# A decoder kernel on one core: the compressed turns placed behind a projection, and part of the first layer's output projection placed ahead of the memory's output

## The chip, the cores and the metric

The kernel runs on one core of one Trainium2 chip. The metric is the time of one execution on the device, in microseconds (us). The kernel before took 633.94 us in the median of three runs (633.56 to 634.37).

The core's engines work through instruction queues of their own, each in order, and wait for each other by semaphores. The profile calls them PE (matrix products; PEld is its loading of weights), DVE (vector), ACT (scalar functions and copies), POOL and SP (which here issues the DMAs).

## The reference: what is computed

Two decoder layers over 256 tokens of width 1024. Each layer has a token mixer, a cross-attention with 4 heads into 256 memory tokens, one output projection of both, and a SwiGLU feed-forward part. The first layer's mixer is a gated MLP; the second's is an attention with three branches.

```python
for i in range(2):
    h, mem_n = rmsnorm(x, norm_mix[i]), rmsnorm(mem, norm_mem[i])
    mix, mem_q = gmlp_mixer(h, ...) if i % 2 == 0 else nsa_mixer(h, ...)
    mem_o = mem_cross_attention(mem_q, mem_n, w_mem_kv[i])      # 4 heads of 64: 256 columns
    x = x + jnp.concatenate([mix, mem_o], axis=-1) @ w_out      # (768 + 256) x 1024
    x = x + swiglu(rmsnorm(x, norm_ffn[i]), wg, wu, wd)
return rmsnorm(x, norm_final)

# nsa_mixer, a head (12 heads of 64, 4 key heads), with softmax p and gate g of each branch:
o = g0 * (p_c @ v_compressed) + g1 * (p_s @ v_selected) + g2 * (p_w @ v_window)
```

With 256 tokens the selected and the window branch both see every earlier position, and the compressed branch sees 15 blocks of keys.

## The kernel before, in words

All matrix products of weights are made three times: a value is held as a rounded high part H and a rest L, and `mm3` (lines 226 to 232) issues H times H (L229), L times H (L230) and H times L (L231). One such triple of 128 rows by 512 columns is called a k-product below. H is made by ACT and L by DVE from the same source (`split`, lines 122 to 124): the L of an activation cannot be made before its H, and the k-product's second matmul needs it. Row tile `tb` is tokens 0 to 127 or 128 to 255.

Weights come through three raw buffers (`Raw`, one DMA from SP each) and seven pairs wH, wL of one piece each; a new piece is cast when the k-product that frees an older one has been recorded (`Stream.pump`). PE's order is the order of the code. Side work is a generator in a heap of due times (`Flow`): `flow.spawn` and each `yield` name a delay, a k-product moves the clock by its estimated length (line 232), and what is due is recorded next. `MEMLAT` is the delay between the scores of the memory attention and the turning of its probabilities. The order on DVE, ACT, POOL and SP is set by a scheduler from the order of the code and from priorities (`tc.high_priority`).

First layer, lines 681 to 707. `v_chain` (lines 650 to 679) makes the mixer's output and turns it for PE (`gm`, L673, transposed by L245). The memory attention (`mem_attention`, lines 382 to 426) runs once per row tile: scores on PE (L389), maxima on DVE (L393), exponentials on ACT (L401), a scaling on POOL (L406), eight transposes on PE (L245), copies on ACT (L414), the products with the values on PE (L422), and the split into the projection's k = 6, 7 (L123 on ACT, L124 on DVE). The output projection `down` (lines 309 to 320) takes k = 0 to 3 for both row tiles and both halves of the columns, waits in the recording until both memory attentions are recorded (line 705), then takes k = 4 to 7. A finished half of a row tile starts `f0.chain` (lines 299 to 303: residual L307, transposes, gain L280, split, squares L250), which the feed-forward part needs.

Second layer, lines 918 to 1074. The 12 heads are taken in six steps m = 0 to 5 of two heads. `scores(m)` needs four of the four PSUM buffers called `tr`; it is followed by masks and maxima on DVE (L945, L947), exponentials on ACT (L951, L963) and the scaling on POOL (L956). `turn(m)` transposes the probabilities of both heads (12 transposes, L245, three `tr` buffers, copied out by ACT at L976 and L982) and then the compressed branch's (`pcx`, one transpose, a fourth `tr` buffer, copied by ACT at L985). `attend(m)` multiplies with the values (L1003), the compressed ones last in each row tile, into a `tr` buffer `o`, which is split for the projection. Between them `mixed` takes pieces (m, tb) of the output projection: two k-products each, k = m, one row tile, both halves. After (5, tb) the chain `f1.chain` is started, and the feed-forward part follows.

Of the kernel before, what the change touches and what calls it, by code (L numbers as in the profile page):

```python
# [58 lines left out]

HI = 150  # L60
UP = 500
MEMLAT = 9.0
MEMCH = 0.0
VCH = 2.0
WARM, WARM2 = 6, 2
# [3 lines left out]
def body(tc, t, out):  # L69
    nc = tc.nc  # L70
    PE, ACT, DVE, POOL, SP = nc.tensor, nc.scalar, nc.vector, nc.gpsimd, nc.sync
    with ExitStack() as ctx:
# [236 lines left out]
        def down(accs, act, ks, ws, first, last, after=None, tbs=(0, 1)):  # L309

            for tb in tbs:
                for half in range(2):
                    acc = accs[tb][half]
                    for i, k in enumerate(ks):
                        mm3(acc, st(act, k, tb), ws[i](slice(half * 512, (half + 1) * 512)),
                            first and i == 0, last and i == len(ks) - 1)
                        if tb == 1 and half == 1:
                            ws[i].done()
                    if after:
                        after(acc, tb, half)  # L320
# [329 lines left out]
        def v_chain():  # L650
            POOL.affine_select(wsr, wsr, pattern=[[0, 12], [-1, 128]], compare_op=ALU.is_ge, fill=0.0, base=0, channel_multiplier=1)
            for tb in range(2):
                ss = tiny([128, 2], "ss")
                sumsq(Vv[:, tb, 0:512], ss[:, 0:1], GW)
                sumsq(Vv[:, tb, 512:768], ss[:, 1:2], GW)
                r = rstd_of(ss)
                yield 1.5
                DVE.scalar_tensor_tensor(Vv[:, tb, :], Vv[:, tb, :], r, vg, op0=ALU.mult, op1=ALU.mult)
            yield 2.0
            for q in range(3):  # L660
                ps = tr()
                transposes(ps, wsr[:, q * 4 : q * 4 + 4, :].rearrange("p g s -> p (g s)"), 4)
                ACT.copy(wsT[:, q * 4 : q * 4 + 4, :], kview(ps, 4))
                yield 0.8 if q < 2 else 2.4
            for q in range(3):
                spatial(q)
                yield 1.0
            for c, n in ((0, 512), (512, 256)):
                for tb in range(2):
                    while tb not in u_done:  # L670
                        yield 0.3
                    gm = small([128, n])
                    DVE.tensor_tensor(gm, U[:, tb, c : c + n], Vv[:, tb, c : c + n], op=ALU.mult)  # L673
                    yield 1.0
                    ps = tr()
                    transposes(ps, gm, n // 128)
                    k = c // 128
                    split(mix[0][:, k : k + n // 128, blk(tb)], mix[1][:, k : k + n // 128, blk(tb)], kview(ps, n // 128))
            v_done.append(1)
# [16 lines left out]
        kv0 = mem_kv(WK0)  # L696
        flow.until(lambda: None not in qT0)
        for tb in range(2):
            flow.spawn(mem_attention(qT0, tb, kv0, mix, mo_done), 1.0 + 5.5 * tb)
        flow.until(lambda: v_done)  # L700
        early.close()
        f0 = Norm(gT[:, FFN : FFN + 8])
        accs = [[mm(), mm()], [mm(), mm()]]
        down(accs, mix, [0, 1, 2, 3], WO0[0] + WO0[1], True, False)
        flow.until(lambda: len(mo_done) == 2)
        down(accs, mix, [4, 5, 6, 7], WO0[2] + WO0[3], False, True,
             lambda *a: flow.spawn(f0.chain(*a)))
        flow.until(lambda: f0.rstd[0] is not None)
        n1 = Norm(gT[:, MIX + 8 : MIX + 16])
        ffn(WF0, f0, n1.chain)  # L710
# [259 lines left out]
        def turn(m):  # L970
            ps = soft[m]
            t0 = tr()
            for hh in range(2):
                transposes(t0, ps[hh], 2, hh * 2)
            pT0 = mid([128, 4, 128])
            ACT.copy(pT0, kview(t0, 4))  # L976
            pT1 = []
            for hh in range(2):
                t1 = tr()
                transposes(t1, ps[hh][:, 256:768], 4)  # L980
                pT1.append(mid([128, 4, 128]))
                ACT.copy(pT1[hh], kview(t1, 4))  # L982
            tc_ = tr()
            transposes(tc_, pcs[:, m % 2], 1)
            ACT.copy(pcT[:, m % 2], tc_[:, 0:128])  # L985
            turned[m] = pT0, pT1

        def attend(m):
            pT0, pT1 = turned[m]
# [26 lines left out]


        def step(f, *a):
            with tc.high_priority(offset=UP if f is turn else HI):
                f(*a)  # L1020

        ps = mm()
# [26 lines left out]
        step(scores, 1)  # L1049
        mixed((6, 1), (7, 1))  # L1050
        step(turn, 0)
        step(scores, 2)
        step(attend, 0)
        step(turn, 1)
        mixed((0, 0))
        step(scores, 3)
        step(attend, 1)
        step(turn, 2)
        mixed((1, 0))
        step(scores, 4)  # L1060
        step(attend, 2)
        step(turn, 3)
        mixed((0, 1))
        step(scores, 5)
        mixed((2, 0))
        step(attend, 3)
        step(turn, 4)
        mixed((1, 1), (3, 0))
        step(attend, 4)
        step(turn, 5)  # L1070
        mixed((2, 1), (4, 0))
        step(attend, 5)
        mixed((3, 1), (5, 0), (4, 1), (5, 1))
        flow.until(lambda: f1.rstd[0] is not None)

        nf = mid2([128, D])
# [63 lines left out]
```

## Time and profile before

| what | value |
|---|---|
| time, median of 3 runs | 633.94 us (633.56 to 634.37) |
| the profiled execution, its own time | 634.55 us |
| its span, first to last instruction | 632.8 us |
| PE busy | 618.1 us, 98% of the span |
| DVE, ACT, POOL busy | 377.1, 327.3, 58.2 us |
| granted TensorE clock, mean | 0.998 of full speed |

The span and the rows are of the one profiled execution; 1.75 us of its time lie outside its span. A timeline row has the start, the length, the engine, the line and operation, what is written from what is read, the shape, the number of merged instructions, and in brackets the engine's idle time just before and what ended it. The length of a matmul overlaps with the next one's; how long PE takes per instruction is read from one start to the next.

### The profile page before, as it was taken

The numbers are of one execution on the slowest core, as the hardware profiler recorded it, in microseconds if no ns is written. First come the engines' busy times: TensorE is split into PE (matmuls) and PEld (weight loads), VectorE is DVE, ScalarE is ACT, GpSimd is POOL, SyncE is SP. The second block draws the span as 40 slices with busy tenths as digits, with TensorE's granted clock in tenths as the row PEclk, the third lists the DMA queues.
The fourth block names the chain that finished last, engine by engine and source line by source line (L and its number), as shares of the span: only waits on it lengthen the run. The fifth ranks groups of instructions, "written<-read, shape, count | busy, mean of one in ns | idle before, by whom it ended". The sixth has DMA issues, their size and how long they took to land.

```text
span 632.8 us, 8848 instructions
## 1 busy us (share of the span) xinstructions
PE 618.1 (98%) x3382; PEld 513.9 (81%) x3382; DVE 377.1 (60%) x616; ACT 327.3 (52%) x553; POOL 58.2 (9%) x90
## 2 busy tenths in 40 slices
PE   8999999999999999999999999899999999999995
PEld 7889879888888888889886787678988888888884
DVE  3998457464554544566688479766544645446344
ACT  4885557452534434456543559766533535344423
POOL 0330121000000000002001204431000000000001
PEclk9999999999999999999999999999999999999999
DMA  7966254555546464643967742133554655647401
GB/s 244 369 217 247 75 165 169 200 172 186 177 171 225 138 261 134 241 159 87 330 201 206 193 103 65 35 121 115 198 199 134 226 173 179 220 138 235 159 1 67
DMA packets 57331, 109.69 MB, mean 173 GB/s; under 512 B 3429, under 2 KB 19401, under 8 KB 57289
## 3 DMA queue, kind: packets, MB, share of 16 engines
q1 hardware_dynamic: 57272, 109.12, 51.9%
q8 instruction: 26, 0.43, 0.3%
q14 instruction: 17, 0.13, 0.1%
q10 hardware_dynamic: 16, 0.00, 0.0%
HBM read 108.07 MB, written 1.05 MB: 172 GB/s over the span
## 4 chain that ended last, share of the span: by engine, by line
PE 90%; ACT 5%; DVE 2%; DMA 1%; issue 1%; POOL 0%; SPq 0%; POOLq 0%; ACTq 0%; DVEq 0%
PE mm L229 14%; PE mm L230 14%; PE mm L231 14%; PE tr L230 13%; PE tr L231 13%; PE tr L229 13%; PE tr L245 5%; ACT mid L951 3%; PE tr L800 1%; DMA x<-in_x_dram 1%; PE tr L389 1%; PE tr L422 1%; PE tr L1003 1%; ACT wH L123 1%; DVE wL L124 0%
## 5 line engine op out<-in xcount | busy, mean ns | idle before, releaser
L124 DVE TENSOR_TENSOR wL<-raw,wH 128x1024 fp32r<-128x1024 f32 (+1 forms) x170 | 205.5, 1228 | 149.5 <-ACT wH L123 143.8
L123 ACT CAST wH<-raw 128x1024 fp32r<-128x1024 f32 (+1 forms) x170 | 173.8, 1043 | 152.3 <-PE tr L230 75.5
L229 PE MATMUL tr<-wH,aH 128*128 128x512 f32 (+1 forms) x384 | 143.8, 375 | 0.0
L230 PE MATMUL tr<-wH,aL 128*128 128x512 f32 (+1 forms) x384 | 142.8, 372 | 0.6 <-DVE aL L124 0.6
L231 PE MATMUL tr<-wL,aH 128*128 128x512 f32 (+1 forms) x384 | 142.7, 372 | 0.0
L229 PE MATMUL mm<-wH,aH 128*128 128x512 f32 (+2 forms) x224 | 87.7, 391 | 0.0
L230 PE MATMUL mm<-wH,aL 128*128 128x512 f32 (+2 forms) x224 | 83.2, 371 | 0.0
L231 PE MATMUL mm<-wL,aH 128*128 128x512 f32 (+2 forms) x224 | 83.2, 371 | 0.0
L230 PEld LDWEIGHTS tr<-wH,aL 128*128 128x128 f32 x384 | 72.4, 188 | 13.0 <-DVE aL L124 0.9
L231 PEld LDWEIGHTS tr<-wL,aH 128*128 128x128 f32 x384 | 72.3, 188 | 12.5
L229 PEld LDWEIGHTS tr<-wH,aH 128*128 128x128 f32 x384 | 72.3, 188 | 12.3
L229 PE MATMUL mm<-wH,mid 128*128 128x512 f32 (+1 forms) x208 | 79.2, 381 | 0.0
L230 PE MATMUL mm<-wH,mid 128*128 128x512 f32 (+1 forms) x208 | 77.9, 374 | 0.0
L231 PE MATMUL mm<-wL,mid 128*128 128x512 f32 (+1 forms) x208 | 77.8, 374 | 0.0
L229 PEld LDWEIGHTS mm<-wH,aH 128*128 128x128 f32 x224 | 42.9, 191 | 9.6 <-issue 4.0
L231 PEld LDWEIGHTS mm<-wL,aH 128*128 128x128 f32 x224 | 42.6, 190 | 7.4
L258 POOL TENSOR_SCALAR rstd<-ss 128x1 f32<-128x1 f32 x14 | 8.0, 575 | 434.6 <-ACT junk L250 430.5
L230 PEld LDWEIGHTS mm<-wH,aL 128*128 128x128 f32 x224 | 42.7, 191 | 5.6
L231 PEld LDWEIGHTS mm<-wL,mid 128*128 128x128 f32 x208 | 39.2, 188 | 7.1
L230 PEld LDWEIGHTS mm<-wH,mid 128*128 128x128 f32 x208 | 39.3, 189 | 6.8 <-DVE mid L124 0.5
L229 PEld LDWEIGHTS mm<-wH,mid 128*128 128x128 f32 x208 | 39.2, 189 | 6.7 <-ACT mid L123 0.4
L453 DVE SCALAR_TENSOR_TENSOR small<-tr,rstd,small 128x512 f32<-128x512 f32 (+1 forms) x24 | 16.9, 703 | 36.5 <-PE tr L231 36.5
(158 smaller groups left out, 652.6 us busy)
## 6 DMA issues: line engine op xcount, KB each, us to landing
raw<-in_ffn_w_down_dram SPq DMA_DIRECT2D x22, 1024.0 KB, 5.1
raw<-in_ffn_w_gate_dram SPq DMA_DIRECT2D x20, 1024.0 KB, 5.2
raw<-in_ffn_w_up_dram SPq DMA_DIRECT2D x20, 1024.0 KB, 5.1
raw<-in_nsa_w_in_dram SPq DMA_DIRECT2D x6, 1024.0 KB, 6.9
raw<-in_gmlp_w_in_dram SPq DMA_DIRECT2D x4, 1024.0 KB, 8.1
raw<-in_w_mem_kv_dram SPq DMA_DIRECT2D x4, 1024.0 KB, 5.8
raw<-in_gmlp_w_out_dram SPq DMA_DIRECT2D x4, 1024.0 KB, 6.2
raw<-in_nsa_w_out_dram SPq DMA_DIRECT2D x12, 256.0 KB, 4.9
```

The source lines that it names most:

```text
L123: ACT.copy(H, src)
L124: DVE.tensor_tensor(L, src, H.bitcast(F32), op=ALU.subtract)
L229: PE.matmul(ps, aH, bH, start=first, stop=False)
L230: PE.matmul(ps, aL, bH, start=False, stop=False)
L231: PE.matmul(ps, aH, bL, start=False, stop=last)
L245: PE.transpose(ps[:, (at + j) * 128 : (at + j + 1) * 128], src[:, j * 128 : (j + 1) * 128], ident)
L258: POOL.tensor_scalar(r, ss[:, 0:1], ss[:, 1:2], EPS, op0=ALU.add, op1=ALU.add)
L389: PE.matmul(scs[i][:, j * 256 : (j + 1) * 256], qT[r, j, :], kv[r, j, :], start=True, stop=True)
L422: PE.matmul(o[i * 64 : i * 64 + 64, blk(j)], kv[:, 2 + b, h : h + 64], pTs[i][:, j * 2 + b, :], start=b == 0, stop=b == 1)
L453: DVE.scalar_tensor_tensor(h, ps[:, :n], nrm.rstd[tb], sil[tb], op0=ALU.mult, op1=ALU.mult)
L800: PE.matmul(ph[s * 64 : s * 64 + 60, 0:256], X[s][:, k // 8, k % 8, :], w1[q, s][:, j, :], start=k == 0, stop=k == 15)
L951: ACT.activation(o, o, AF.Exp, bias=nb[:, i : i + 1], scale=-1.0, accum_out=sm[:, i : i + 1])
```

## The change

`MEMLAT` goes from 9 to 8, the second memory attention is spawned 3.5 instead of 5.5 after the first, and the transposes of `gm` come due 2.0 instead of 1.0 after its product. The first layer's projection is recorded in three parts: k = 4, 5 of row tile 0 ahead of the point that waits for the memory attention, then k = 6, 7 of row tile 0, then k = 4 to 7 of row tile 1. In the second layer the compressed transpose and its copy leave `turn` and become `turn_c`, which is recorded behind a piece of the projection in each step but the first. At m = 4 `turn_c` stands between the pieces (1, 1) and (3, 0). Of the projection's pieces (4, 0) moves behind the last `attend`, and (3, 1) behind (5, 0): (4, 0), (5, 0), (3, 1), (4, 1), (5, 1) stand there instead of (3, 1), (5, 0), (4, 1), (5, 1).

```diff
--- before.py
+++ after.py
@@ -59,7 +59,7 @@
 
 HI = 150
 UP = 500
-MEMLAT = 9.0
+MEMLAT = 8.0
 MEMCH = 0.0
 VCH = 2.0
 WARM, WARM2 = 6, 2
@@ -671,7 +671,7 @@
                         yield 0.3
                     gm = small([128, n])
                     DVE.tensor_tensor(gm, U[:, tb, c : c + n], Vv[:, tb, c : c + n], op=ALU.mult)
-                    yield 1.0
+                    yield 2.0
                     ps = tr()
                     transposes(ps, gm, n // 128)
                     k = c // 128
@@ -696,15 +696,17 @@
         kv0 = mem_kv(WK0)
         flow.until(lambda: None not in qT0)
         for tb in range(2):
-            flow.spawn(mem_attention(qT0, tb, kv0, mix, mo_done), 1.0 + 5.5 * tb)
+            flow.spawn(mem_attention(qT0, tb, kv0, mix, mo_done), 1.0 + 3.5 * tb)
         flow.until(lambda: v_done)
         early.close()
         f0 = Norm(gT[:, FFN : FFN + 8])
         accs = [[mm(), mm()], [mm(), mm()]]
         down(accs, mix, [0, 1, 2, 3], WO0[0] + WO0[1], True, False)
+        down(accs, mix, [4, 5], WO0[2], False, False, None, (0,))
         flow.until(lambda: len(mo_done) == 2)
-        down(accs, mix, [4, 5, 6, 7], WO0[2] + WO0[3], False, True,
-             lambda *a: flow.spawn(f0.chain(*a)))
+        after = lambda *a: flow.spawn(f0.chain(*a))
+        down(accs, mix, [6, 7], WO0[3], False, True, after, (0,))
+        down(accs, mix, [4, 5, 6, 7], WO0[2] + WO0[3], False, True, after, (1,))
         flow.until(lambda: f0.rstd[0] is not None)
         n1 = Norm(gT[:, MIX + 8 : MIX + 16])
         ffn(WF0, f0, n1.chain)
@@ -980,10 +982,12 @@
                 transposes(t1, ps[hh][:, 256:768], 4)
                 pT1.append(mid([128, 4, 128]))
                 ACT.copy(pT1[hh], kview(t1, 4))
-            tc_ = tr()
-            transposes(tc_, pcs[:, m % 2], 1)
-            ACT.copy(pcT[:, m % 2], tc_[:, 0:128])
             turned[m] = pT0, pT1
+
+        def turn_c(m):
+            t = tr()
+            transposes(t, pcs[:, m % 2], 1)
+            ACT.copy(pcT[:, m % 2], t[:, 0:128])
 
         def attend(m):
             pT0, pT1 = turned[m]
@@ -1016,7 +1020,7 @@
 
 
         def step(f, *a):
-            with tc.high_priority(offset=UP if f is turn else HI):
+            with tc.high_priority(offset=UP if f in (turn, turn_c) else HI):
                 f(*a)
 
         ps = mm()
@@ -1049,28 +1053,35 @@
         step(scores, 1)
         mixed((6, 1), (7, 1))
         step(turn, 0)
+        step(turn_c, 0)
         step(scores, 2)
         step(attend, 0)
         step(turn, 1)
         mixed((0, 0))
+        step(turn_c, 1)
         step(scores, 3)
         step(attend, 1)
         step(turn, 2)
         mixed((1, 0))
+        step(turn_c, 2)
         step(scores, 4)
         step(attend, 2)
         step(turn, 3)
         mixed((0, 1))
+        step(turn_c, 3)
         step(scores, 5)
         mixed((2, 0))
         step(attend, 3)
         step(turn, 4)
-        mixed((1, 1), (3, 0))
+        mixed((1, 1))
+        step(turn_c, 4)
+        mixed((3, 0))
         step(attend, 4)
         step(turn, 5)
-        mixed((2, 1), (4, 0))
+        mixed((2, 1))
+        step(turn_c, 5)
         step(attend, 5)
-        mixed((3, 1), (5, 0), (4, 1), (5, 1))
+        mixed((4, 0), (5, 0), (3, 1), (4, 1), (5, 1))
         flow.until(lambda: f1.rstd[0] is not None)
 
         nf = mid2([128, D])
```

PE's order in the first layer, from the first transposes of a memory attention's probabilities whose products follow at once (`tr<-ident,small` x8 are transposes, L422 the products with the memory's values, L229 to L231 the k-products). Before:

```order
L245 MATMUL tr<-ident,small 128x128 x8
L229 MATMUL mm<-wH,aH 128x512
L230 MATMUL mm<-wH,aL 128x512
L231 MATMUL mm<-wL,aH 128x512
L422 MATMUL tr<-small,memkv 64x128 x8
L245 MATMUL tr<-ident,small 128x128 x8
L422 MATMUL tr<-small,memkv 64x128 x8
L229 MATMUL mm<-wH,aH 128x512
L230 MATMUL mm<-wH,aL 128x512
L231 MATMUL mm<-wL,aH 128x512
```

In the change, the same place:

```order
L245 MATMUL tr<-ident,small 128x128 x8
L422 MATMUL tr<-small,memkv 64x128 x8
L229 MATMUL mm<-wH,aH 128x512
L230 MATMUL mm<-wH,aL 128x512
L231 MATMUL mm<-wL,aH 128x512
L229 MATMUL mm<-wH,aH 128x512
L230 MATMUL mm<-wH,aL 128x512
L231 MATMUL mm<-wL,aH 128x512
L422 MATMUL tr<-small,memkv 64x128 x8
L229 MATMUL mm<-wH,aH 128x512
```

The eight transposes of the second row tile's probabilities have moved ahead of the first row tile's L422, two k-products have come between the two L422, and four more stand ahead of this place than before.

ACT's order at the same place, from the last exponentials' successor on (`wH` are weights, `small<-tr` the copies L414 of turned probabilities, `aH` the high part of the memory's output, first for row tile 0, then 1; raw_919 and raw_933 hold the first part of the feed-forward `up` weights, raw_646 the projection's last two pieces). Before:

```order
L123 CAST wH_915<-raw_646 128x1024
L123 CAST wH_938<-raw_789 128x1024
L414 COPY small_929<-tr_924 128x512
L414 COPY small_936<-tr_931 128x512
L123 CAST wH_947<-raw_811 128x1024
L123 CAST aH_429<-tr_953 128x2x128
L414 COPY small_969<-tr_964 128x512
L414 COPY small_976<-tr_971 128x512
L123 CAST wH_992<-raw_919 128x1024
L123 CAST aH_429<-tr_978 128x2x128
```

In the change:

```order
L123 CAST wH_929<-raw_646 128x1024
L414 COPY small_917<-tr_912 128x512
L414 COPY small_924<-tr_919 128x512
L123 CAST wH_938<-raw_789 128x1024
L123 CAST wH_947<-raw_811 128x1024
L414 COPY small_970<-tr_965 128x512
L414 COPY small_977<-tr_972 128x512
L123 CAST wH_956<-raw_933 128x1024
L123 CAST aH_429<-tr_979 128x2x128
L123 CAST aH_429<-tr_996 128x2x128
```

The cast of row tile 0's output has moved from ahead of the last weight cast, the one from the `up` weights, to behind it. DVE's order follows it: row tile 0's aL stood behind three wL and stands behind four.

PE's order in the attention stage at step m = 4 (`mid_` with a number are the two heads' probabilities, `pcx` the compressed ones). Before:

```order
L245 MATMUL tr<-ident,mid_3840 128x128 x4
L245 MATMUL tr<-ident,mid_3857 128x128 x4
L245 MATMUL tr<-ident,pcx 128x128
L229 MATMUL mm<-wH,aH 128x512
L230 MATMUL mm<-wH,aL 128x512
L231 MATMUL mm<-wL,aH 128x512
L229 MATMUL mm<-wH,aH 128x512
```

In the change:

```order
L245 MATMUL tr<-ident,mid_3840 128x128 x4
L245 MATMUL tr<-ident,mid_3857 128x128 x4
L229 MATMUL mm<-wH,aH 128x512
L230 MATMUL mm<-wH,aL 128x512
L231 MATMUL mm<-wL,aH 128x512
L229 MATMUL mm<-wH,aH 128x512
L230 MATMUL mm<-wH,aL 128x512
L231 MATMUL mm<-wL,aH 128x512
L245 MATMUL tr<-ident,pcx 128x128
L229 MATMUL mm<-wH,aH 128x512
```

The compressed transpose has moved behind one piece of the projection, which is (1, 1) here.

ACT's order at the last step, m = 5 (L976, L982 and L985 of before are L978, L984 and L990 in the change). Before:

```order
L976 COPY mid<-tr 128x512
L982 COPY mid<-tr 128x512 x2
L985 COPY pcx<-tr 128x128
L123 CAST wH<-raw 128x1024
L123 CAST aH<-tr 128x256
```

In the change:

```order
L978 COPY mid<-tr 128x512
L984 COPY mid<-tr 128x512 x2
L123 CAST wH<-raw 128x1024
L990 COPY pcx<-tr 128x128
L123 CAST aH<-tr 128x256
```

The compressed copy has moved behind a weight cast, which waits for the k-products of the piece that now stands ahead of the compressed transpose.

## Rows read from the trace of the kernel before

**Rows 1.** The page's first part: busy time of each engine, share of the span and number of instructions.

```profile
PE 618.1 (98%) x3382; PEld 513.9 (81%) x3382; DVE 377.1 (60%) x616; ACT 327.3 (52%) x553; POOL 58.2 (9%) x90
```

**Rows 2.** The waits of TensorE by what ended them, whole span: engine, line, waited for; us in total, times, the longest in us.

```profile
PE tr L245 <- DVE aL L124: 2.5, 3, 1.0
PE tr L230 <- DVE aL L124: 0.6, 1, 0.6
...
PE tr L422 <- ACT small L414: 0.2, 1, 0.2
```

**Rows 3.** Timeline of TensorE in the first layer, where the memory attention and the projection meet (start, length, operation, shape, merged instructions, idle before).

```profile
77.99 0.50 PE L229 MATMUL mm<-wH,aH 128*128 128x512 f32 x1
...
82.21 1.03 PE L245 MATMUL tr<-ident,small 128*128 128x128 f32 x8
...
83.55 0.40 PE L231 MATMUL mm<-wL,aH 128*128 128x512 f32 x1
84.09 1.57 PE L422 MATMUL tr<-small,memkv 128*64 128x128 f32 x16
85.60 1.09 PE L245 MATMUL tr<-ident,small 128*128 128x128 f32 x8
86.93 1.58 PE L422 MATMUL tr<-small,memkv 128*64 128x128 f32 x16 [0.24 <-ACT small L414]
88.43 0.50 PE L229 MATMUL mm<-wH,aH 128*128 128x512 f32 x1
...
91.29 0.39 PE L229 MATMUL mm<-wH,aH 128*128 128x512 f32 x1
```

**Rows 4.** Timeline of TensorE at the second layer's memory attention: the same products L422 and what follows them.

```profile
354.86 1.09 PE L422 MATMUL tr<-small,memkv 128*64 128x128 f32 x16
355.88 0.50 PE L229 MATMUL mm<-wH,aH 128*128 128x512 f32 x1
```

**Rows 5.** Timeline of the other engines in the first layer, from the second row tile's maxima on (SPq is SP's queue, which issues the DMAs).

```profile
79.48 0.23 POOL L395 TENSOR_SCALAR nb<-mx 128x4 f32<-128x4 f32 x1 [0.53 <-DVE mx L393]
...
82.64 4.63 DVE L124 TENSOR_TENSOR wL<-raw,wH 128x1024 fp32r<-128x1024 f32 x3 [0.76 <-ACT wH L123]
...
84.18 2.35 SPq L153 DMA_DIRECT2D raw<-in_ffn_w_up_dram  x2
...
89.53 1.05 ACT L123 CAST wH<-raw 128x1024 fp32r<-128x1024 f32 x1 [2.17 <-DMA raw<-in_ffn_w_up_dram]
90.49 0.37 ACT L123 CAST aH<-tr 128x256 fp32r<-128x256 f32 x1
90.62 1.23 DVE L124 TENSOR_TENSOR wL<-raw,wH 128x1024 fp32r<-128x1024 f32 x1 [3.01 <-ACT wH L123]
91.76 0.42 DVE L124 TENSOR_TENSOR aL<-tr,aH 128x256 fp32r<-128x256 f32 x1
```

**Rows 6.** DMA issues: what is loaded, queue, count, KB each, median us from issue to landing.

```profile
raw<-in_ffn_w_up_dram SPq DMA_DIRECT2D x4, 512.0 KB, 4.3
...
raw<-in_nsa_w_in_dram SPq DMA_DIRECT2D x4, 512.0 KB, 8.4
```

**Rows 7.** Timeline of DVE and TensorE at the transposes of `gm` in the first layer.

```profile
57.21 0.48 DVE L693 TENSOR_SCALAR small<-mm,rstd 128x256 f32<-128x256 f32 x1
57.43 0.85 PE L245 MATMUL tr<-ident,small 128*128 128x128 f32 x6 [0.21 <-DVE small L673]
```

**Rows 8.** Timeline of TensorE in the attention stage and at the start of the feed-forward part behind it.

```profile
395.94 0.33 PE L245 MATMUL tr<-ident,pcx 128*128 128x128 f32 x1 [0.55 <-ACT mid L976]
...
396.34 0.42 PE L230 MATMUL mm<-wH,aL 128*128 128x512 f32 x1
...
403.95 0.33 PE L245 MATMUL tr<-ident,pcx 128*128 128x128 f32 x1 [0.99 <-DVE aL L124]
...
404.35 0.40 PE L230 MATMUL mm<-wH,aL 128*128 128x512 f32 x1
...
411.77 0.33 PE L245 MATMUL tr<-ident,pcx 128*128 128x128 f32 x1 [1.00 <-DVE aL L124]
...
420.63 0.33 PE L245 MATMUL tr<-ident,pcx 128*128 128x128 f32 x1 [0.48 <-DVE aL L124]
...
427.95 0.39 PE L230 MATMUL mm<-wH,aL 128*128 128x512 f32 x1
...
429.88 0.66 PE L1003 MATMUL tr<-mid,V 128*64 128x128 f32 x8
430.37 0.39 PE L1003 MATMUL tr<-pcx,vc 128*64 128x128 f32 x4
...
438.52 0.28 PE L229 MATMUL tr<-wH,aH 128*128 128x256 f32 x1
439.37 0.39 PE L230 MATMUL tr<-wH,aL 128*128 128x256 f32 x1 [0.58 <-DVE aL L124]
```

**Rows 9.** Timeline of DVE and ACT in the attention stage.

```profile
395.80 0.41 DVE L124 TENSOR_TENSOR aL<-tr,aH 128x256 fp32r<-128x256 f32 x1
...
403.49 0.41 DVE L124 TENSOR_TENSOR aL<-tr,aH 128x256 fp32r<-128x256 f32 x1
...
427.73 0.30 ACT L985 COPY pcx<-tr 128x128 f32<-128x128 f32 x1
428.38 1.05 ACT L123 CAST wH<-raw 128x1024 fp32r<-128x1024 f32 x1 [0.35 <-PE mm L230]
```

## The prediction

> **What bounds the kernel.** I read the busy times first: TensorE is busy 618.1 of 632.8 us [rows 1], so a change of order pays only where it removes idle time of TensorE, some 14.7 us in all. The view of TensorE's waits says where that is [rows 2]: 2.5 us in three waits of a transpose (L245) for DVE's aL, 0.6 us in one wait of L230 for aL, 0.2 us of L422 for ACT's copies. The timeline places them: the three long ones stand ahead of the compressed transposes of steps m = 2, 3 and 4, that of L230 at the start of the feed-forward part [rows 8], that of L422 in the first layer [rows 3]. A fourth `tr` buffer is needed by the compressed transpose, and its holder, the `o` of the attend before, is given free by the split, whose last part is aL. The change deals with just these places.
>
> The unit of the sums: six k-products and nothing else lie between 77.99 and 82.21 [rows 3], so one takes 4.22/6 = 0.70 us and each of its three matmuls 0.23.
>
> **First layer.** In before a matmul that starts at 83.55 is followed by L422 at 84.09, 0.31 us late (0.54 less 0.23). The first L422 group takes until 85.60 (1.51), the second from 86.93 to 88.43 (1.50) [rows 3]; the same products take 355.88 − 354.86 = 1.02 in the second layer [rows 4], so 0.49 are lost in each. The eight transposes take 0.79 (82.21 to the next product at 83.00, about what ends at 86.39), and 86.93 − 85.60 − 0.79 = 0.54 is waited for. Sum 0.31 + 0.49 + 0.54 + 0.49 = 1.83 us. In the change at least one group of products of 0.70 stands between each group of transposes and its L422, and the first row tile's transposes lie far ahead: I take all 1.83 as gone. Cut short by nothing else, TensorE would come to the first product of k = 6 (row tile 0, twelve products left) 1.7 us before its 91.29 of before [rows 3], at about 89.6 (0.11 goes for one more change between products and transposes).
>
> But that product's L230 needs row tile 0's aL, and the order puts it behind the fourth weight cast and its wL, which is where row tile 1's aL stood. In before that place was late: the raw buffer's DMA was issued at 84.18, the cast began at 89.53 after 2.17 us of waiting for it, aH came at 90.49, wL at 90.62, and aL ended at 91.76 + 0.42 = 92.18 [rows 5]. What leads to the issue hardly moves: the second row tile's scores come three products earlier, but its maxima's next step on POOL (79.48 [rows 5]) stands behind the first tile's scaling and gains some 0.15 us, no more; then the same exponentials, cast and wL follow. So aL is ready at 92.18 − 0.15 = 92.03. L229 of that product is through by then, L230 waits, and the product stands as if begun at 92.03 − 0.23 = 91.8, against 91.29: **a loss of 0.5 us** where the waits removed were worth 1.8. The new wait is about 2.1 us. The residual chain of row tile 0 then has eight products of row tile 1 to hide behind and adds nothing.
>
> The bounds of this term: if the data came at once, +1.7. The landing, about 5.3 us here (84.18 to 89.53), is 4.3 in the median of its kind and 8.4 for another load of 512 KB [rows 6]; 8.4 would make the loss 0.5 + 3.1 = 3.6. I take 5.3, the row of that very DMA.
>
> The Trainium skill (page "SBUF — State Buffer", section "The DMA setup-cost knee (why "@ 1 MiB" ≠ asymptote)") gives a transfer a fixed 2 us or so and its bytes over 436 GB/s. For 512 KB that is an estimate by that page of 3.2 us; the trace does not agree, since its rows say 4.3 in the median and 5.3 here. By the page aL would be there 2.1 us earlier, at the very time TensorE comes to it, and the first layer would gain 1.7 instead of losing 0.5.
>
> The transposes of `gm` that waited for L673 change places with transposes of the queries, which read what L693 writes: that ends at 57.21 + 0.48 = 57.69, after the 57.43 at which the waiting group starts [rows 7]. One wait of 0.2 to 0.4 takes the place of another: 0, within 0.2. At the second layer's memory attention only the number of products between transposes and L422 changes, and no wait stands there [rows 4]: 0, within 0.2.
>
> **Attention stage, step by step.** m = 0 keeps its order. At m = 1 the piece (0, 0) now follows the turn at once; its L230 needs the aL of attend 0, which ends at 395.80 + 0.41 = 396.21 [rows 9], and L230 ran at 396.34 already [rows 8]: 0. At m = 2 the piece (1, 0) needs the aL of attend 1, ended at 403.49 + 0.41 = 403.90 [rows 9], the same event that freed the compressed transpose at 403.95. So the wait of 0.99 changes its name; L230 goes at 403.95 instead of 404.35 [rows 8], and the transpose follows later, at 0.1: +0.3. At m = 3 the piece is (0, 1), whose aL is long made. Its two products (1.4 us) cover the wait of 1.00 before 411.77 [rows 8] with the change between products and transposes (0.16): +1.15. At m = 4 the piece (1, 1) covers the 0.48 (0.64 with that change) before 420.63: +0.6.
>
> At m = 5 the change costs. ACT's queue has the weight cast ahead of the compressed copy now, and the cast waits for the second L230 of the piece (2, 1), 427.95 [rows 8]. It began at 428.38 and lasts 1.05, the copy 0.30 [rows 9]; without the transpose ahead all is 0.11 earlier, so pcT is ready at about 429.6. Attend 5 stands directly behind now, not two products later, and starts at 427.95 + 0.46 = 428.4; it wants pcT 430.37 − 429.88 = 0.49 later [rows 8], at 428.9: −0.65. Behind the wait is only the rest of attend 5, and its split.
>
> At the end, row tile 0's chain has four products in front of the first gate product instead of two, 1.4 us more, since (3, 1) follows (5, 0). The wait at 438.52 to 439.37 (0.85 less 0.12 to the next matmul of this width, 0.73) [rows 8] and one of 0.1 to 0.2 among the residual's transposes go: +0.8. aL comes just in time, so not more.
>
> Together 0 + 0.3 + 1.15 + 0.6 − 0.65 + 0.8 = **+2.2 us**. Below, the step's loop (scores, masks, exponentials, turn) may hold instead of TensorE, and the gains of m = 2 to 4 fall away: then +0.15. Above, without the loss at m = 5, +2.9.
>
> **Sum.** −0.5 + 0 + 2.2 = 1.7 us less. The profiled execution took 634.55, which gives 632.85; it lies 0.61 above the runs' median of 633.94, so I predict 632.2 us.
>
> **Rivals.** *No wait at k = 6*: the `up` weights land in time. The gain is 1.7 + 2.2 = 3.9 and about 630.0, or 630.4 with part of a wait. For it speaks the median of 4.3, one us less [rows 6]; against it that very DMA's own row. 13%.
> *The waits only change their names in the attention stage*: with TensorE ahead, scores come earlier, but exponentials and casts of ACT do not follow, and the next turn is late by what was gained. That m = 2's wait does just that speaks for it; against it, that TensorE waits for ACT's probabilities only 0.6 us before m = 1's compressed transpose [rows 8], not before those of m = 3 to 5. −0.5 + 0.15 = −0.35 or, with the loss at m = 5 hidden, zero: 633.9 to 634.3, say 633.9. 25%.
> *Slower*: one mechanism, the landing of the `up` weights on which row tile 0's aL now depends. At 8.4 instead of 5.3 the first layer loses 3.6, and the whole is 1.4 slower: 635.3. The whole turns to loss at 5.3 + 1.7 = 7.0, and shows from 8.3. A landing that long stands in the trace for another load, so 7%.
> *Forecast*: 55%, 632.2, its own range 631.2 to 633.2.
>
> A measurement of this kernel tells 0.2% (1.27 us) from no change: faster is below 632.67, slower above 635.21. The forecast puts some four fifths of its 55% below 632.67, the first rival all of its 13%, the second none: faster 0.57; same 0.36, from the rest of the forecast and the second rival; slower 0.07. For 8 in 10 the range runs from 630.5, which leaves out half of the first rival, to 634.5, past the second rival's upper end of 634.3 and short of the third.
>
> **What would show it.** In the changed kernel's trace: no wait at L422 and some 2 us before an L230 of the first layer, ended by DVE's aL; L230 waits for aL at m = 1 and 2; no idle time before the compressed transposes of m = 3 and 4; some 0.65 inside attend 5, ended by ACT's compressed copy; no wait for aL at the first gate product. Wrong would be an L230 of k = 6 that doesn't wait, or scores and turns of m = 4 and 5 that stand no earlier than in before, counted from the stage's start.

## The result, and the profile after

The changed kernel took 629.37 us in the median of four runs (629.09 to 631.13) against 633.75 of before (633.00 to 634.37): ratio 0.9937, 95% interval 0.9916 to 0.9959. It is faster, by 4.4 us, where 1.7 were forecast (632.2, range 630.5 to 634.5). The sign was right; the size was not.

Its profiled execution took 629.09 us, 5.46 less than that of before. The head of its page, and TensorE's waits over the whole span (engine, line, what was waited for; us in total, times, longest):

```profile
span 627.4 us, 8848 instructions
PE 615.9 (98%) x3382; PEld 511.5 (82%) x3382; DVE 375.2 (60%) x616; ACT 327.9 (52%) x553; POOL 58.0 (9%) x90
```

```profile
PE tr L245 <- DMA x<-in_x_dram: 1.4, 2, 0.9
PE tr L112 <- DVE warm L103: 1.1, 1, 1.1
PE mm L230 <- DVE aL L124: 0.7, 2, 0.4
PE tr L929 <- ACT mid L978: 0.5, 1, 0.5
PE tr L1007 <- ACT pcx L990: 0.4, 1, 0.4
PE tr L1007 <- DVE pcx L947: 0.3, 1, 0.3
PE tr L245 <- DVE small L693: 0.2, 1, 0.2
```

The 2.5 us of the transposes that waited for aL, the 0.6 of L230 at the first gate product behind the attention and the 0.2 of L422 [rows 2] are gone. Two waits of L230 for aL, which by the timeline stand at m = 1 and m = 2 (0.30 and 0.42), and one of attend 5 for the compressed copy are new. The wait at k = 6 isn't in this list; it is read from the starts below. (In the changed kernel L929, L931, L933 are the scores that were L927, L929, L931, and L1007 is attend, L1003 before.)

**The first layer.** TensorE, where the products of row tile 0's k = 6 begin, the place of [rows 3]:

```profile
83.05 1.03 PE L245 MATMUL tr<-ident,small 128*128 128x128 f32 x8
84.02 1.09 PE L422 MATMUL tr<-small,memkv 128*64 128x128 f32 x16
85.04 0.50 PE L229 MATMUL mm<-wH,aH 128*128 128x512 f32 x1
...
86.63 1.09 PE L422 MATMUL tr<-small,memkv 128*64 128x128 f32 x16
87.66 0.49 PE L229 MATMUL mm<-wH,aH 128*128 128x512 f32 x1
88.25 0.50 PE L230 MATMUL mm<-wH,aL 128*128 128x512 f32 x1
```

Both groups of L422 take 1.02 and 1.03 us instead of 1.5, without a wait ahead of them. L230 starts 0.59 behind its L229; after the same change of operation at 85.04 it starts 0.34 behind (85.38), so 0.25 us is waited for. The forecast had 2 us there. The other engines, the place of [rows 5]:

```profile
81.65 2.35 SPq L153 DMA_DIRECT2D raw<-in_ffn_w_up_dram  x2
85.55 1.05 ACT L123 CAST wH<-raw 128x1024 fp32r<-128x1024 f32 x1 [0.79 <-DMA raw<-in_ffn_w_up_dram]
86.51 0.36 ACT L123 CAST aH<-tr 128x256 fp32r<-128x256 f32 x1
86.64 1.22 DVE L124 TENSOR_TENSOR wL<-raw,wH 128x1024 fp32r<-128x1024 f32 x1 [1.90 <-ACT wH L123]
87.78 0.82 DVE L124 TENSOR_TENSOR aL<-tr,aH 128x256 fp32r<-128x256 f32 x2
```

The chain is the forecast's, link by link: load, cast, wL, aL (87.78, two of 0.41), L230 at 88.25. Only the load is shorter: the cast starts 3.90 us after the issue, 5.35 in before.

**The attention stage.** TensorE and ACT at m = 3 of the changed kernel:

```profile
408.19 0.27 PE L245 MATMUL tr<-ident,pcx 128*128 128x128 f32 x1
408.39 0.73 PE L929 MATMUL tr<-KT,QT 64*128 64x271 f32 x4
408.96 0.29 PE L931 MATMUL tr<-KT,QT 64*128 64x15 f32 x4
409.10 1.75 PE L933 MATMUL tr<-KT,QT 64*128 64x512 f32 x4
410.78 0.50 PE L229 MATMUL mm<-wH,aH 128*128 128x512 f32 x1
```

```profile
408.46 1.05 ACT L123 CAST wH<-raw 128x1024 fp32r<-128x1024 f32 x1
409.41 0.27 ACT L990 COPY pcx<-tr 128x128 f32<-128x128 f32 x1
```

The transpose at 408.19 has no wait ahead of it, as forecast (1.00 in before, [rows 8]). But the four L933 take 1.68 us (409.10 to 410.78). In before the same four took 1.04:

```profile
414.12 1.11 PE L931 MATMUL tr<-KT,QT 64*128 64x512 f32 x4
415.16 0.50 PE L229 MATMUL mm<-wH,aH 128*128 128x512 f32 x1
```

No idle time is shown there. The two heads' products use 64 rows of the array each and run side by side: single records of before start in pairs 0.01 us apart. The second head's need a fourth `tr` buffer, which the compressed copy frees at 409.68, and the copy stands behind a weight cast on ACT. By the single records the second head's start at 409.73, 0.63 behind the first head's, and the group is longer by as much. Since the first head's are running meanwhile, it looks like work. The Trainium skill ("TensorE: Matmul & The Clock Gate", section "Part 3: Packing small matmuls — row/col tiling") says that products in different row groups of the array run at the same time; the trace agrees, with 1.04 us where the two heads start together and 1.68 where one starts 0.63 later.

TensorE and ACT at m = 5, in the same kernel:

```profile
423.46 0.66 PE L1007 MATMUL tr<-mid,V 128*64 128x128 f32 x8
424.50 0.44 PE L1007 MATMUL tr<-pcx,vc 128*64 128x128 f32 x4 [0.37 <-ACT pcx L990]
```

```profile
423.23 1.04 ACT L123 CAST wH<-raw 128x1024 fp32r<-128x1024 f32 x1 [0.41 <-PE mm L230]
424.18 0.26 ACT L990 COPY pcx<-tr 128x128 f32<-128x128 f32 x1
```

The compressed products come 1.04 behind attend 5's start, 0.49 in before [rows 8]: 0.55 lost. At the start of the feed-forward part L230 follows its L229 at once, where 0.85 lay between them [rows 8]:

```profile
433.79 0.28 PE L229 MATMUL tr<-wH,aH 128*128 128x256 f32 x1
433.90 0.38 PE L230 MATMUL tr<-wH,aL 128*128 128x256 f32 x1
```

**Where the 5.4 us between the two spans lie**, by TensorE's starts in the two timelines (before, after): up to the first memory scores 70.88 and 68.79, so 2.09; from there to L230 of the first gate product 30.14 and 29.09, so 1.05; then the feed-forward part and the second layer up to the first scores 276.59 and 276.12, so 0.47; from the first scores to L230 of the second gate product 61.76 and 59.90, so 1.86; the rest agrees within 0.03. The second and the fourth hold nearly all that the change does. The 2.09 come ahead of nearly all that it touches, and are looked at first below.

### The profile page after: what moved, and what is told of

It reads as the page before. It is cut to its first block, busy times and chain, and to the rows that moved or that the text cites. A ratio compares the mean times of both kernels' runs of the same rounds, so it can differ in the third digit from the quotient of the medians.

```text
span 627.4 us, 8848 instructions
## 1 busy us (share of the span) xinstructions
PE 615.9 (98%) x3382; PEld 511.5 (82%) x3382; DVE 375.2 (60%) x616; ACT 327.9 (52%) x553; POOL 58.0 (9%) x90
## 3 DMA queue, kind: packets, MB, share of 16 engines
HBM read 108.07 MB, written 1.05 MB: 174 GB/s over the span
## 4 chain that ended last, share of the span: by engine, by line
PE 91%; ACT 4%; DVE 2%; DMA 2%; issue 0%; SPq 0%; POOL 0%; POOLq 0%; ACTq 0%
PE mm L229 14%; PE mm L230 14%; PE mm L231 14%; PE tr L230 13%; PE tr L231 13%; PE tr L229 13%; PE tr L245 5%; ACT mid L953 2%; PE tr L1007 1%; PE tr L802 1%; DMA x<-in_x_dram 1%; DVE wL L124 1%; PE tr L389 1%; ACT wH L123 1%; DMA raw<-in_ffn_w_up_dram 1%
## 5 line engine op out<-in xcount | busy, mean ns | idle before, releaser
L229 PE MATMUL tr<-wH,aH 128*128 128x512 f32 (+1 forms) x384 | 143.8, 375 | 0.0
L230 PE MATMUL tr<-wH,aL 128*128 128x512 f32 (+1 forms) x384 | 142.8, 372 | 0.0
L231 PE MATMUL tr<-wL,aH 128*128 128x512 f32 (+1 forms) x384 | 142.7, 372 | 0.0
L229 PE MATMUL mm<-wH,aH 128*128 128x512 f32 (+2 forms) x224 | 86.8, 388 | 0.1
L230 PE MATMUL mm<-wH,aL 128*128 128x512 f32 (+2 forms) x224 | 83.0, 371 | 0.8 <-DVE aL L124 0.7
L231 PE MATMUL mm<-wL,aH 128*128 128x512 f32 (+2 forms) x224 | 82.9, 370 | 0.0
L231 PEld LDWEIGHTS tr<-wL,aH 128*128 128x128 f32 x384 | 72.3, 188 | 12.5
L230 PEld LDWEIGHTS tr<-wH,aL 128*128 128x128 f32 x384 | 72.4, 188 | 12.3
L229 PEld LDWEIGHTS tr<-wH,aH 128*128 128x128 f32 x384 | 72.3, 188 | 12.3
L229 PE MATMUL mm<-wH,mid 128*128 128x512 f32 (+1 forms) x208 | 79.3, 381 | 0.0
L230 PE MATMUL mm<-wH,mid 128*128 128x512 f32 (+1 forms) x208 | 77.8, 374 | 0.0
L231 PE MATMUL mm<-wL,mid 128*128 128x512 f32 (+1 forms) x208 | 77.8, 374 | 0.0
L229 PEld LDWEIGHTS mm<-wH,aH 128*128 128x128 f32 x224 | 42.2, 188 | 10.1 <-issue 4.0
L230 PEld LDWEIGHTS mm<-wH,aL 128*128 128x128 f32 x224 | 42.3, 189 | 7.6 <-DVE aL L124 2.1
L231 PEld LDWEIGHTS mm<-wL,aH 128*128 128x128 f32 x224 | 42.1, 188 | 7.6 <-DVE wL L129 0.4
L231 PEld LDWEIGHTS mm<-wL,mid 128*128 128x128 f32 x208 | 39.2, 188 | 7.1
L230 PEld LDWEIGHTS mm<-wH,mid 128*128 128x128 f32 x208 | 39.3, 189 | 6.9 <-DVE mid L124 0.5
L229 PEld LDWEIGHTS mm<-wH,mid 128*128 128x128 f32 x208 | 39.2, 188 | 6.7 <-ACT mid L123 0.4
```

The costliest lines, as they stand in the source:

```text
L229: PE.matmul(ps, aH, bH, start=first, stop=False)
L230: PE.matmul(ps, aL, bH, start=False, stop=False)
L231: PE.matmul(ps, aH, bL, start=False, stop=last)
```

## The experiments

**Both kernels again, for their traces.** Before and after unchanged.

> The kernel before, unchanged, once more, for its trace. The trace of before lost 2.05 us in the first 12 us, where an x row landed at 6.60 us (5.74 in the trace of after) and the next matmuls ran 0.43 apart instead of 0.23; nothing in the change touches that place. Theory 1 (a lottery of every execution): some executions of this kernel have the early start and are about 2 us shorter; the ratio to before is 1.000. Theory 2 (the change shifts it): no execution of this kernel has it. For the load of the up weights in the first layer: theory A (it was a late landing by chance) expects less than 5.3 us here, about 4; theory B (5.3 belongs to the order of before, whose two loads follow closer to other traffic) expects 5.0 to 5.5 again.

> The changed kernel once more, for its trace. Expected 629.1 to 631.1, the early start in some of its executions and the late one in others (theory 1), or the early one in all (theory 2). The wait of the first k = 6 product for aL was 0.36 us with a landing of 3.8 us; if the landing is 5.3 here (theory A), the wait is 1.8 and the kernel 1.5 longer in that stage.

Before: 633.61 us (632.27 to 634.95, 12 runs), ratio to before 1.0003 (0.9995 to 1.0011). After: 631.18 us (629.28 to 632.00, 6 runs) against 633.38, ratio 0.9962 (0.9947 to 0.9976). In this trace of before the first memory scores come at 68.94, within 0.15 us of the first trace of after; in the second trace of after they come at 69.95. So the 2.09 us were the draw of one execution (theory 1), and so was the landing of 5.3 us (theory A): it is 3.6 here, in the same order. The start of the two traces of before, first the one that the prediction rests on, then the other:

```profile
6.64 1.12 PE L245 MATMUL tr<-ident,x 128*128 128x128 f32 x4 [1.36 <-DMA x<-in_x_dram]
7.55 1.06 PE L112 MATMUL tr<-warm 128*128 128x128 f32 x4
8.26 0.77 PE L229 MATMUL mm<-wH,aH 128*128 128x512 f32 x1
8.84 0.63 PE L230 MATMUL mm<-wH,aL 128*128 128x512 f32 x1
9.26 0.63 PE L231 MATMUL mm<-wL,aH 128*128 128x512 f32 x1
```

```profile
5.48 1.11 PE L245 MATMUL tr<-ident,x 128*128 128x128 f32 x4 [0.20 <-DMA x<-in_x_dram]
6.38 0.86 PE L112 MATMUL tr<-warm 128*128 128x128 f32 x4
7.00 0.48 PE L229 MATMUL mm<-wH,aH 128*128 128x512 f32 x1
...
9.73 0.44 PE L245 MATMUL tr<-ident,x 128*128 128x128 f32 x2 [1.01 <-DMA x<-in_x_dram]
```

The input's part landed late in the first, TensorE waited 1.36 instead of 0.20 us, and the matmuls that followed ran 0.42 us apart (8.84 to 9.26) where 0.23 is usual. The second trace waits for another part of the input later, 1.01 us at 9.73, so the waits come to nearly the same in both; what differs is the pace. The view by stretches has that of 8 to 10 us of the first trace so (length; busy time and count of PE, PEld, DVE, ACT, POOL; granted clock, DMA share, GB/s):

```profile
8.00:10.00 2.00, 2.00 (x7) 1.71 (x7) 1.37 (x2) 1.49 (x3) 0.00 (x0) 1.00 1.03 393
```

The granted clock reads 1.00, but nothing was recorded there. The trace's list of granted clocks begins at 12.50 us in the first trace and at 6.90 in the second, each time with the higher of the clock's two levels, and the view counts what lies ahead of the list as 1.00; so does the mean of 0.998 in the table of before. In all twelve traces the pace changes where the list begins, at 4.48 to 12.78 us: ahead of it transposes of 128x128 start 0.21 us apart and products of 128x512, where there are any, 0.43, behind it 0.11 and 0.23. By this pace the stretch ahead ran at the lower level. The three traces whose list begins after 10 us (before, `attn_only`, `first_halves`) have the three latest first memory scores of the table below. What sets the moment isn't shown: TensorE waited 0.50 us for this part of the input in after and 0.52 in `attn_only`, and their lists begin at 5.22 and 10.34.

**Half the change alone.** `attn_only` is the changed kernel with the first layer's lines (MEMLAT, the spawn, the yield of `gm`, the split projection) set back; `first_only` is before with just these lines.

> Only the second layer's part of the change: turn_c behind a piece, and the order of the last pieces. The traces of before and after differ by 1.1 us from the first scores to the first gate product and by 0.7 behind it, so 1.85 us less than before: about 631.9 (ratio 0.997). Were the gain only in the first layer or in the start, 633.7 (ratio 1.000).

> Only the first layer's part of the change, with MEMLAT, the earlier spawn, the later gm transposes and the projection in three parts. By the traces 1.5 us less between the first memory scores and the second layer's first scores: about 632.2 (ratio 0.9976). By my forecast's step (aL waits 2 us at k = 6) 0.5 us more than before: 634.2 (1.0008). If what is gained lay in the start alone, 633.7.

`attn_only`: 631.91 us (11 runs), ratio 0.9977 (0.9968 to 0.9985), 1.5 us less. `first_only`: 632.46 (11 runs), ratio 0.9986 (0.9977 to 0.9994), 0.9 less. Both halves gain, and together, 2.4 us, they come near the 2.2 that the second measurement of the whole change shows, not to 4.4. The 0.5 us more that my step asked of the first layer isn't there. Nor are the 1.5 less that the first two traces let expect of `first_only`; its traced load took 4.6 us, against 3.8 in the first trace of after.

**The changed kernel a third time.**

> The changed kernel a third time, for its time and its trace. By the stages that repeat (1.86 us less in the attention stage; between 1.0 less and 0.1 less in the first layer as the up load lands 3.8 or 4.8 us after its issue, 0.5 more at 5.3) the change is worth 2.0 to 2.9 us: ratio 0.9955 to 0.9968, some 631. If the 4.4 us of its first measurement were its true worth, 629.3 (0.993).

630.64 us (629.71 to 630.83, 5 runs) against 633.40: ratio 0.9954 (0.9942 to 0.9967). The ratios of the three measurements are 0.9937, 0.9962 and 0.9954; the median of the 15 executions is 630.64. The first measurement had three of its four executions between 629.09 and 629.60; of the eleven later ones only one lies as low. The three intervals overlap; by the 15 executions together the change is worth some 2.8 us, and their median lies just inside the range of 630.5 to 634.5.

**The split ahead of the cast.** In the first layer one weight cast is recorded later, and the order of this stretch on ACT and DVE is held as recorded.

```diff
-                while self.live < AHEAD and self.split < len(self.pieces):
+                while self.live < AHEAD - self.hold and self.split < len(self.pieces):
...
+        stream.hold = 1
         down(accs, mix, [0, 1, 2, 3], WO0[0] + WO0[1], True, False)
...
+        with tc.manual_schedule(engines={mybir.EngineType.DVE, mybir.EngineType.Activation}):
+            down(accs, mix, [4, 5], WO0[2], False, False, None, (0,))
+            flow.until(lambda: len(mo_done) == 2)
+            stream.hold = 0
+            down(accs, mix, [6, 7], WO0[3], False, True, after, (0,))
```

> The changed kernel with one exchange on ACT and DVE: the split of both row tiles' memory outputs stands ahead of the cast of the first up weights, and wL behind aL. Theory A (the first layer's term is set by that load's landing): no wait at k = 6 whatever the load does; from the first memory scores to the first gate product 28.4 to 28.8 us (30.13 in before, 29.09 with a landing of 3.83 us and 30.04 with 4.81 in the changed kernel), so 0.3 to 1.6 less than the changed kernel. Rival B (the wait at k = 6 is for TensorE's own L422 or the copies, not the load): that stretch again follows the landing, 29.1 at 3.8 and 30.0 at 4.8.

629.31 us (6 runs) against 633.50, ratio 0.9941 (0.9925 to 0.9957). The stretch from the first memory scores to the first gate product takes 28.71 us with a landing of 4.4: theory A. ACT and TensorE of this kernel (its lines are one higher):

```profile
86.09 0.37 ACT L123 CAST aH<-tr 128x256 fp32r<-128x256 f32 x1 [0.40 <-PE tr L423]
88.71 0.37 ACT L123 CAST aH<-tr 128x256 fp32r<-128x256 f32 x1 [2.24 <-PE tr L423]
88.98 1.05 ACT L123 CAST wH<-raw 128x1024 fp32r<-128x1024 f32 x1
```

```profile
87.57 1.09 PE L423 MATMUL tr<-small,memkv 128*64 128x128 f32 x16
88.59 0.50 PE L230 MATMUL mm<-wH,aH 128*128 128x512 f32 x1
88.93 0.39 PE L231 MATMUL mm<-wH,aL 128*128 128x512 f32 x1
```

aH of row tile 0 follows its own L423, and the second matmul of the k = 6 product comes 0.34 behind the first, without a wait.

**The transpose between the two products of its piece**, at m = 3 and m = 5 (`mixed` and `down` get a parameter `halves`, not shown here):

```diff
-        mixed((0, 1))
+        mixed((0, 1), halves=(0,))
         step(turn_c, 3)
+        mixed((0, 1), halves=(1,))
...
-        mixed((2, 1))
+        mixed((2, 1), halves=(0,))
         step(turn_c, 5)
+        mixed((2, 1), halves=(1,))
```

> The changed kernel with the compressed transpose of m = 3 and m = 5 placed between the two k-products of its piece instead of behind both; on ACT this puts the compressed copy ahead of the weight cast at both places and changes nothing else there. Theory C (the cast ahead of the copy costs 0.65 at m = 3, through the fourth buffer that scores 5 need, and 0.6 at m = 5, in attend 5): from the first scores to the second gate product 58.8 to 59.2 us instead of 59.9, scores 5 again with both heads' last products side by side. Rival D (scores 5 lose it to something of their own, the masks or the maxima): attend 3 begins 3.98 us behind scores 5 as in the changed kernel, only the 0.6 of m = 5 goes, 59.3.

629.34 us (6 runs), ratio 0.9935 (0.9921 to 0.9950). From the first scores to the second gate product 59.17 us; attend 3 begins 3.33 behind scores 5, not 3.98. ACT and TensorE at m = 3 of this kernel:

```profile
409.49 0.26 ACT L990 COPY pcx<-tr 128x128 f32<-128x128 f32 x1
409.81 1.05 ACT L123 CAST wH<-raw 128x1024 fp32r<-128x1024 f32 x1
```

```profile
408.99 0.33 PE L245 MATMUL tr<-ident,pcx 128*128 128x128 f32 x1 [0.29 <-DVE aL L124]
...
410.64 1.11 PE L933 MATMUL tr<-KT,QT 64*128 64x512 f32 x4
411.68 0.50 PE L229 MATMUL mm<-wH,aH 128*128 128x512 f32 x1
```

The copy is ahead of the cast and the four L933 take 1.04 again: theory C. At m = 5 the compressed products come 0.49 behind attend 5's start again (424.38, 424.87). But at m = 3 one product doesn't cover all of the wait for aL: 0.29 of it is back, scores 5 begin 0.50 later than in the changed kernel, and attend 3 only 0.14 earlier. Of the 0.73 that the stage gains, 0.57 come behind the start of attend 4.

**Two pieces exchanged.**

```diff
-        mixed((1, 0))
+        mixed((0, 1))
         step(turn_c, 2)
...
-        mixed((0, 1))
+        mixed((1, 0))
         step(turn_c, 3)
```

> The changed kernel with the pieces (1, 0) and (0, 1) exchanged: m = 2 takes (0, 1), which needs nothing of the step, and m = 3 takes (1, 0). Theory: the wait of m = 2, which only changed its name to L230 (0.8 us with what stands around it), goes, and so does the 0.65 at m = 3, since (1, 0) frees no weight piece and brings no cast ahead of the copy; but the cast comes ahead of the copy at m = 2 now, which gives 0.65 back at scores 4: 59.1 us from the first scores to the gate product, 0.8 less than the changed kernel. Rival E (the loop of scores, exponentials and turn sets the step, and waits in it only move): 59.9 again, with a new wait for ACT's probabilities at the next turn.

630.57 us (6 runs), ratio 0.9953 (0.9938 to 0.9969); the stage takes 59.88 us, as in the changed kernel. TensorE and ACT at m = 2:

```profile
401.98 1.75 PE L933 MATMUL tr<-KT,QT 64*128 64x512 f32 x4
404.32 0.66 PE L1007 MATMUL tr<-mid,V 128*64 128x128 f32 x8 [0.59 <-DVE pcx L947]
```

```profile
401.35 1.05 ACT L123 CAST wH<-raw 128x1024 fp32r<-128x1024 f32 x1
402.29 0.27 ACT L990 COPY pcx<-tr 128x128 f32<-128x128 f32 x1
```

Scores 4 come 1.0 us earlier, and the cast ahead of the copy takes 0.65 of it, as expected; then attend 2 waits 0.59 for DVE's mask of the compressed scores, which I hadn't seen, and begins 0.24 later than in the changed kernel. At m = 3 the 0.65 is gained as expected, so that attend 3 begins 0.40 earlier, and by attend 4 that is gone too. By its number rival E is right, by its place it named the wrong engine.

**Corrections together.** `first_halves` joins the edits of `split_first` and `halves`. `first_halves_swap` also exchanges the two pieces, with the transpose of m = 2 between the products of (0, 1).

> Both corrections in one kernel: the memory's split ahead of the up weights' cast, and the compressed transposes of m = 3 and m = 5 between the two products of their pieces. From the first memory scores to the first gate product 28.7 us whatever the load does, from the first scores to the second gate product 59.17: some 1.4 less than the changed kernel where the load takes 4.4, and 2.7 plus 1.4 = 4.0 less than before in these two stages.

> The kernel first_halves with (1, 0) and (0, 1) exchanged too, and the compressed transpose of m = 2 between the two products of (0, 1). The exchange alone gave nothing, since scores 4 met the cast ahead of the copy (0.65) and then the mask of the compressed scores (L947, 0.59). Here the cast is behind the copy at every step: theory, 0.4 to 0.8 less than first_halves in the attention stage, 58.4 to 58.8; rival (the step's loop holds: masks, exponentials, turn), 59.2 again with the waits at other places.

`first_halves`: 628.97 us (628.16 to 630.42, 5 runs) against 633.40, ratio 0.9927 (0.9914 to 0.9941); measured beside it, the changed kernel took 630.64. Its two stages take 28.70 and 59.18 us, 4.0 less than before together, as expected. It has the lowest median, 1.7 us below the changed kernel. Its interval overlaps with those of `split_first` and `halves`: that the two gains add up is shown by the stages, not by the medians. `first_halves_swap`: 629.87, ratio 0.9941 (0.9928 to 0.9953), with 28.67 and 59.60: the exchange costs 0.4 where it was to give 0.4 to 0.8 and where the rival expected no change. In its trace scores 4 come 0.51 earlier than in `first_halves`; attend 2 then waits 1.04 for DVE's mask of the compressed scores, which stands behind a wL until 403.46, and begins 0.59 later. So something other than TensorE holds the step, as the rival has it, but the loss is in neither expectation.

**The twelve traces, by stage.** Times are differences of TensorE's starts; the load is the first of the `up` weights, from issue to landing.

| kernel | first memory scores at | `up` load | to L230 of the first gate product | first scores to L230 of the second |
|---|---|---|---|---|
| before | 70.88 | 5.3 | 30.14 | 61.76 |
| before_again | 68.94 | 3.6 | 30.13 | 61.75 |
| attn_only | 70.58 | 3.5 | 30.13 | 59.88 |
| first_only | 69.99 | 4.6 | 29.81 | 61.75 |
| after | 68.79 | 3.8 | 29.09 | 59.90 |
| after_again | 69.95 | 4.8 | 30.04 | 59.89 |
| after_third | 69.68 | 4.6 | 29.84 | 59.91 |
| swap_pieces | 69.24 | 4.0 | 29.25 | 59.88 |
| halves | 69.99 | 3.6 | 28.86 | 59.17 |
| split_first | 69.73 | 4.4 | 28.71 | 59.88 |
| first_halves | 70.97 | 4.2 | 28.70 | 59.18 |
| first_halves_swap | 68.63 | 3.5 | 28.67 | 59.60 |

In the order of before the stretch from the first memory scores to L230 of the first gate product doesn't depend on the load (30.13 to 30.14 at 3.5 to 5.3). In the changed order it does, one for one (28.86 at 3.6, 30.04 at 4.8). With the split ahead of the cast it doesn't again. What makes the load land after 3.5 or after 5.3 us isn't shown.

## Why the prediction was wrong

**The start: not a term of the sum, and 2.1 us of the traces' difference.** Twelve executions of an almost unchanged stretch reach the first memory scores between 68.63 and 70.97 us. The prediction took its own trace as typical but for 0.61 us; that trace had the second latest start of the twelve, and the trace of after the second earliest. The two profiled executions lie 5.46 apart where 1.7 were forecast; of the 3.8 more, 2.1 are the start, 1.55 the first layer's term (+1.05 for −0.5), 0.5 the part between the stages and −0.3 the attention stage. That a like draw separates the 4.4 of the first measurement from the 2.2 and 2.8 us of the two later ones is likely; of its four executions only one was traced.

**The first layer: the step that failed.** It is the sentence "I take 5.3, the row of that very DMA". The mechanism was right: the order puts row tile 0's aL behind the cast of the `up` weights, and L230 waits for it. The size was off: 5.3 is the longest of twelve landings; their median is about 4.1, near the 4.3 of the kind [rows 6]. So the term is a gain of 0.1 to 1.3 us at landings of 4.8 to 3.6, and by the same slope 0.8 at the median of 4.1. At 5.3 the slope gives a loss of 0.4, where −0.5 was worked out; no trace of the changed order has so late a landing. The removed waits were 1.7 in the working, one more change of operation taken off, and make 1.43 where nothing else waits (30.14 − 28.71). The estimate of 3.2 us by the Trainium skill (page "SBUF — State Buffer", section "The DMA setup-cost knee (why "@ 1 MiB" ≠ asymptote)"), which I set aside, lies below all twelve; the nearest are 3.5 and 3.6. The rival that came nearest, "No wait at k = 6", which allowed part of a wait at 630.4, stood at 13%. With 4.3, the median of the kind, in place of 5.3 the same working gives +0.5 for the term, 2.7 in all and 631.2.

**A smaller link.** The issue of that load moved by 0.44 us against the first memory scores (13.30 to 12.86), where 0.15 was worked out.

**The attention stage: 1.86 of the 2.2, in every trace.** By cumulative starts from the first scores: m = 1, −0.1 for 0; m = 2, +0.3 for +0.3; m = 3 up to scores 5, +1.2 for +1.15; m = 4, +0.65 for +0.6; m = 5 and the end, +0.45 for +0.15 (−0.55 of attend 5 and, as the remainder, +1.0 of the chain, for −0.65 and +0.8). Between scores 5 and attend 3 0.66 is lost that the working didn't have: at m = 3 as at m = 5 the cast comes ahead of the compressed copy on ACT. I looked for what the copy holds up at m = 5, where the product that reads it follows at once, and not at m = 3, where it holds a buffer.

**The `gm` transposes.** The wait for L673 became one for L693 as said, but of 0.2 to 1.1 us over the traces; `attn_only`, in the old order, waits 1.0 there as well, and both traces of before 0.2. Whether the new order makes the long wait likelier, three traces of the old one can't tell. What it costs falls into the start.

**The second layer's memory attention.** 0, within 0.2, as said: from L422 to the first scores the nine traces of the new order take 22.66 us and the three of the old 22.75. The rest of the 0.47 between the first two traces stands ahead of L422, in a stretch that differs by 0.35 between traces of one kernel.

## What to carry to other kernels

When a step becomes dependent on a DMA, its price is the spread of that load over executions, and one profiled execution gives one draw of it; take the median of the kind, keep the one row as an end. When an instruction moves behind another on an in-order queue, ask of it twice: who reads what it writes, and whose buffer it frees. A stage whose length repeats within 0.03 us from trace to trace settles what a median over executions that differ by 2 us cannot.

## What the runs showed that was not expected

Products of two heads that run side by side lose their pairing when one of them has to wait for a buffer, 1.68 us for 1.04, and the views of waits show nothing, since the engine is busy. And a clock of 1.00 in a view can stand for no record: ahead of the first entry of the list of granted clocks, which comes at 4.48 to 12.78 us here, TensorE ran at half its later pace in every trace, 0.21 us for 0.11 from one 128x128 transpose to the next, and the view by stretches shows none of it.
